# Rotary scores on one core: stores of 128 rows split into 112, 15 and 1 rows in half of the steps, with k's transposes moved late

## The chip, the cores and the metric

The kernel runs on one core of one Trainium2 chip. The time is the device time of the whole program in microseconds (us), as the median of its runs. Spans in profiles are about 1.8 us shorter than times. The ratios are taken over fast runs of both kernels; they differ a little from the ratio of the medians quoted beside them.

## The reference, cut to what matters

```python
batch, seq, heads, dim = 16, 512, 16, 64          # fp32 throughout
q_rot = concat([q1 * cos - q2 * sin, q1 * sin + q2 * cos])   # the halves of dim; k likewise
scores = np.einsum('bshd,bthd->bsht', q_rot, k_rot)
```

The last line means: `out[b, s, h, t]` is the product of the rotated q at (s, h) with the rotated k at (t, h). The output has 16 x 512 x 16 x 512 fp32 numbers, 268 MB, and q and k are 67 MB together. So the kernel is mostly a matter of writing.

## The kernel before

There are 64 steps, four for each batch. A step computes the scores of 128 positions: VectorE rotates q and k, TensorE transposes them and multiplies, ScalarE copies the scores from PSUM into a staging tile of 128 rows by 32 KB, and one DMA issued by SyncE stores the tile. There are three staging tiles.

```python
stage_pool = ctx.enter_context(tc.tile_pool(name="stage", bufs=3))
# ... cut ...
def scores(i, p, st):
    # ... cut: two matmuls into ps ...
    nc.scalar.copy(out=st[:, 2 * p : 2 * p + 2, :], in_=ps)
    if b == 0 and p % 2 == 1:                       # the first four steps: in quarters
        nc.sync.dma_start(o_v[0, c, :, G * i : G * (i + 1)], st[:, G * c : G * (c + 1)])
    elif b > 0 and p == HP - 1:                     # the other 60 steps: one DMA of 128 rows
        nc.sync.dma_start(o_v[b, i % C], st)
# ... cut ...
for i in range(C, NST):
    # ... cut: load of a later pair of q or k ...
    for p in range(HP):
        scores(i, p, st)
        if p in (0, 2, 3, 5) and tr:                # k's transposes first, then q's
            bank, dst = transposed(*tr.pop(0))
            run(dve[:1]); dve = dve[1:]
            nc.vector.tensor_copy(out=dst, in_=bank)
```

## Time and profile before

| | before |
|---|---|
| time, median of 2 | 811.86 us (811.51 to 812.21) |
| span of the profiled run | 810.0 us |
| bytes moved by SyncE's DMA queue | 335.55 MB, its packets fill 98.1% of the 16 DMA engines' span |
| TensorE busy | 676.1 us (83%) |
| mean rate | 415 GB/s |

The third and fourth rows say what to read first: the DMA engines have no room (98.1%), every compute engine has some (the busiest, TensorE, is at 83%). The page counts 16 DMA engines, and the trace holds 16 completion records for each of the 148 DMAs of this kernel. I read each record as one engine's, so the spread of the 16 shows how far the engines have drifted apart. Each packet has a duration too. Both kinds of records are in the trace.

### The profile page before, as it was taken

How to read it: one execution, taken by the hardware profiler on the slowest of the kernel's cores; microseconds unless marked ns; L12 is line 12 of the kernel's file. 1: busy time of each engine (PE TensorE's matmuls, PEld its weight loads, DVE VectorE, ACT ScalarE, POOL GpSimd, SP SyncE). 2: the span in 40 equal slices, each digit the busy share in tenths (PEclk: the TensorE clock that was granted, in tenths of full speed). 3: DMA queues.
4: the chain of work that ended last, by engine and by line, in shares of the span. 5: the costliest groups of instructions: out<-in, count | busy, mean ns of one | idle time of the engine just before them, and what ended most of it. 6: DMA issues, size and time to landing. Idle time of an engine off the chain costs nothing.

```text
span 810.0 us, 7781 instructions
## 1 busy us (share of the span) xinstructions
PE 676.1 (83%) x3072; PEld 297.1 (37%) x3072; DVE 598.7 (74%) x624; ACT 500.1 (62%) x533; POOL 0.7 (0%) x6
## 2 busy tenths in 40 slices
PE   4997999888887888978888888888888889889960
PEld 2443444333333333333333333333333334334310
DVE  7798988877777877868868688677778787786300
ACT  3884777656565675566666656665656657566770
POOL 0000000000000000000000000000000000000000
PEclk9998999999999999999999999999999999999995
DMA  8999999999999999999999999999999999999994
GB/s 272 383 424 397 426 428 426 433 418 431 434 424 432 433 422 434 433 421 438 431 420 437 432 420 438 432 420 438 432 417 442 409 421 440 428 386 435 398 417 202
DMA packets 29028, 336.31 MB, mean 415 GB/s; under 512 B 3392, under 2 KB 7744, under 8 KB 15424
## 3 DMA queue, kind: packets, MB, share of 16 engines
q1 hardware_dynamic: 27648, 335.55, 98.1%
q8 instruction: 24, 0.39, 0.2%
q10 hardware_dynamic: 1344, 0.26, 0.2%
q14 instruction: 12, 0.10, 0.0%
HBM read 67.37 MB, written 268.44 MB: 415 GB/s over the span
## 4 chain that ended last, share of the span: by engine, by line
DMA 58%; PE 22%; DVE 8%; ACT 8%; issue 1%; ACTq 0%
DMA out_dram<-st 57%; PE ps L159 16%; ACT st L166 8%; PE bank L136 6%; DVE part L118 3%; DVE k_rot L121 2%; DVE k_rot L115 1%; DVE q_rot L121 1%; DVE q_rot L115 1%; DVE qT_t L259 1%; DMA sin_k<-in_sin_dram 1%; DVE kT_t L215 0%; ACT kT_t L176 0%; ACTq L286 0%; ACTq L166 0%
## 5 line engine op out<-in xcount | busy, mean ns | idle before, releaser
L166 ACT COPY st<-ps 128x1024 f32<-128x1024 f32 x512 | 488.9, 1022 | 275.0 <-DMA out_dram<-st 176.4
L159 PE MATMUL ps<-kT_t,qT_t 64*128 64x512 f32 x2048 | 528.0, 637 | 72.1 <-ACT st L166 69.4
L159 PEld LDWEIGHTS ps<-kT_t,qT_t 64*128 64x128 f32 x2048 | 183.6, 194 | 255.3 <-issue 148.3
L259 DVE COPY qT_t<-bank 128x512 f32<-128x512 f32 x118 | 81.6, 691 | 135.7 <-PE bank L136 135.1
L136 PE MATMUL bank<-ident,k_rot 128*128 128x128 f32 x512 | 84.6, 291 | 35.7 <-DVE k_rot L121 35.6
L136 PEld LDWEIGHTS bank<-ident,k_rot 128*128 128x128 f32 x512 | 55.1, 143 | 132.7 <-DVE k_rot L121 69.0
L136 PEld LDWEIGHTS bank<-ident,q_rot 128*128 128x128 f32 x512 | 58.4, 149 | 99.8 <-issue 74.8
L259 DVE COPY kT_t<-bank 128x512 f32<-128x512 f32 x112 | 77.0, 688 | 24.2 <-PE bank L136 24.2
L136 PE MATMUL bank<-ident,q_rot 128*128 128x128 f32 x512 | 90.0, 304 | 1.9 <-DVE q_rot L121 1.9
L121 DVE TENSOR_TENSOR k_rot<-k_rot,part 128x1024 f32<-128x1024 f32 x64 | 78.4, 1224 | 2.1
L115 DVE TENSOR_TENSOR q_rot<-q_sb,cos_q 128x1024 f32<-128x1024 f32 x64 | 78.0, 1219 | 0.0
L121 DVE TENSOR_TENSOR q_rot<-q_rot,part 128x1024 f32<-128x1024 f32 x64 | 77.8, 1216 | 0.2
L118 DVE TENSOR_TENSOR part<-q_sb,ss_q 128x1024 f32<-128x1024 f32 x64 | 77.8, 1216 | 0.0
L115 DVE TENSOR_TENSOR k_rot<-k_sb,cos_k 128x1024 f32<-128x1024 f32 x64 | 77.8, 1216 | 0.0
L118 DVE TENSOR_TENSOR part<-k_sb,ss_k 128x1024 f32<-128x1024 f32 x64 | 77.8, 1216 | 0.0
L176 ACT COPY kT_t<-bank 128x512 f32<-128x512 f32 x10 | 5.6, 619 | 6.6 <-PE bank L136 6.6
L215 DVE COPY kT_t<-bank 128x512 f32<-128x512 f32 x6 | 4.1, 685 | 4.5 <-PE bank L136 4.5
L176 ACT COPY qT_t<-bank 128x512 f32<-128x512 f32 x10 | 5.6, 618 | 2.6 <-PE bank L136 2.6
L59 DVE COPY ss_k<-sin_k 128x128 f32<-128x128 f32 x1 | 0.2, 227 | 5.3 <-DMA sin_k<-in_sin_dram 5.3
L176 ACT ACT_TABLE_LOAD x1 | 1.3, 1283 | 2.9 <-issue 2.9
masks.py:199 POOL TENSOR_SCALAR_AFFINE_SELECT ident<-ident 128x128 f32<-128x128 f32 x1 | 0.3, 292 | 0.1
L60 DVE TENSOR_SCALAR ss_q<-sin_q 128x128 f32<-128x128 f32 x1 | 0.2, 222 | 0.0
(7 smaller groups left out, 1.0 us busy)
## 6 DMA issues: line engine op xcount, KB each, us to landing
out_dram<-st SPq DMA_DIRECT2D x60, 4096.0 KB, 28.1
k_sb<-in_k_dram SPq DMA_DIRECT2D x30, 1024.0 KB, 19.1
q_sb<-in_q_dram SPq DMA_DIRECT2D x30, 1024.0 KB, 27.2
out_dram<-st SPq DMA_DIRECT2D x16, 1024.0 KB, 9.9
k_sb<-in_k_dram SPq DMA_DIRECT2D x4, 512.0 KB, 7.0
q_sb<-in_q_dram SPq DMA_DIRECT2D x4, 512.0 KB, 8.4
cos_k<-in_cos_dram ACTq DMA_DIRECT2D x1, 64.0 KB, 4.2
sin_k<-in_sin_dram ACTq DMA_DIRECT2D x1, 64.0 KB, 4.1
```

The costliest lines, as they stand in the source:

```text
L59: nc.vector.tensor_copy(out=ss[:, :, 0, :], in_=tabs["sin", which])
L60: nc.vector.tensor_scalar_mul(ss[:, :, 1, :], tabs["sin", which], -1.0)
L115: lambda: nc.vector.tensor_tensor(a.rearrange(v1, **k1), src.rearrange(v1, **k1), cs, op=mult),
L118: lambda: nc.vector.tensor_tensor(bt.rearrange(v1, **k2), src.rearrange(v1, **k2), ss, op=mult),
L121: lambda: nc.vector.tensor_tensor(a4, a4, swapped, op=add),
L136: nc.tensor.transpose(bank[:, x, :], src, ident)
L159: nc.tensor.matmul(out=ps[:, r, :], lhsT=lhs[64 * r : 64 * r + 64, :], rhs=rhs[64 * r : 64 * r + 64, :], start=True, stop=True,)
L166: nc.scalar.copy(out=st[:, 2 * p : 2 * p + 2, :], in_=ps)
L176: nc.scalar.copy(out=dst, in_=bank)
L215: nc.vector.tensor_copy(out=dst, in_=bank)
L259: nc.vector.tensor_copy(out=dst, in_=bank)
```

## The change

The name of the change says that it comes on top of another one, "k's transposes late and moved by ScalarE". Four things differ. The first loads go into a staging-sized tile of their own in larger pieces, and more loads are issued at the start. The sine tables are built by ScalarE. k's transposes come late in a step and ScalarE copies them out. And in 33 of the 60 whole stores (steps 12 to 44) rows 0 to 111 are stored by SyncE, rows 112 to 126 by GpSimd, and row 127 by two DMAs of 16 pieces of 1 KB. The aim of the last part is probably to take a row off one of the 16 DMA engines: the trace has one packet of 32 KB a row, so the 112 rows could be 7 for each, and the 15 packets of GpSimd's DMA leave at least one engine without one.

```diff
+    MIXED = range(12, 45)
+    early = stage_pool.tile([P, 2 * C * H * D], fp32, tag="stage", name="early")
 ...
+    def store(o, st, mixed):
+        if not mixed:
+            nc.sync.dma_start(o, st)
+            return
+        n = P - 16
+        nc.sync.dma_start(o[:n], st[:n])
+        nc.gpsimd.dma_start(o[n : P - 1], st[n : P - 1])
+        o = o[P - 1 :].rearrange("p h (x t) -> p x h t", x=2)
+        last = st[P - 1 :].rearrange("p h (x t) -> p x h t", x=2)
+        for x in range(2):
+            nc.sync.dma_start(o[:, x], last[:, x])
 ...
-            nc.sync.dma_start(o_v[b, i % C], st)
+            store(o_v[b, i % C], st, i in MIXED)
 ...
-            tr = []
+            tr = {}
+            if i + 1 < NST:
+                tr[1], tr[3] = ("q", i + 1, 0), ("q", i + 1, 1)
             if i + C < NST:
-                tr += [("k", i + C, g) for g in range(2)]
+                tr[5], tr[6] = ("k", i + C, 0), ("k", i + C, 1)
 ...
+                if tr[p][0] == "q":
+                    nc.vector.tensor_copy(out=dst, in_=bank)
+                else:
+                    nc.scalar.copy(out=dst, in_=bank)
```

More of the change, by code (lines that the diff above doesn't have):

```diff
@@ L58, in build_table @@
         ss = const_pool.tile([P, C, 2, HD], fp32, name=f"ss_{which}")
-        nc.vector.tensor_copy(out=ss[:, :, 0, :], in_=tabs["sin", which])
-        nc.vector.tensor_scalar_mul(ss[:, :, 1, :], tabs["sin", which], -1.0)
+        nc.scalar.copy(out=ss[:, :, 0, :], in_=tabs["sin", which])
+        nc.scalar.mul(ss[:, :, 1, :], tabs["sin", which], -1.0)
         tabs["ss", which] = ss.rearrange("p c x j -> p c (x j)")
@@ L71, in in_tile, with load_units @@
         return t
-    def load_unit(which, u):
-        t = in_tiles.get((which, u // 2))
-        if t is None:
-            t = in_tile(which, u // 2)
-        src = (k_v if which == "k" else q_v)[0, :, :, G * u : G * (u + 1), :]
-        nc.sync.dma_start(t[:, u % 2].rearrange("p (c h d) -> p c h d", c=C, h=G), src)
+    st_first = [stage_pool.tile([P, H, S], fp32, tag="stage", name="st") for _ in range(2)]
+    early = stage_pool.tile([P, 2 * C * H * D], fp32, tag="stage", name="early")
+    units = {}
+    def load_units(which, head, heads):
+        n = C * heads * D
+        t = early[:, load_units.used : load_units.used + n]
+        load_units.used += n
+        t = t.rearrange("p (c e) -> p c e", c=C)
+        src = (k_v if which == "k" else q_v)[0, :, :, head : head + heads, :]
+        nc.sync.dma_start(t.rearrange("p c (h d) -> p c h d", d=D), src)
+        for h in range(0, heads, G):
+            units[which, (head + h) // G] = t[:, :, D * h : D * (h + G)]
+    load_units.used = 0
     def load_pair(which, pair):
@@ L92, in rope @@
     def rope(which, n):
-        src = in_tiles[which, n // 2][:, n % 2]
         a = rot_pool.tile([P, H * D], fp32, tag="rot_" + which, name=which + "_rot")
@@ L99, in rope @@
         if n < C:
+            src = units[which, n]
+            sv = "p c (g j) -> p c g j"
             v1 = "p (c g j) -> p c g j"
@@ L105, in rope @@
         else:
+            src = in_tiles[which, n // 2][:, n % 2]
+            sv = "p (g j) -> p g j"
             v1 = "p (g j) -> p g j"
@@ L115, in rope @@
             lambda: nc.vector.tensor_tensor(
-                a.rearrange(v1, **k1), src.rearrange(v1, **k1), cs, op=mult
+                a.rearrange(v1, **k1), src.rearrange(sv, j=HD), cs, op=mult
             ),
             lambda: nc.vector.tensor_tensor(
-                bt.rearrange(v1, **k2), src.rearrange(v1, **k2), ss, op=mult
+                bt.rearrange(v1, **k2), src.rearrange(sv, j=D), ss, op=mult
             ),
@@ L184 @@
         load_tables("q", "(p c) j -> p c j")
-        for u in range(2):
-            load_unit("k", u)
-            load_unit("q", u)
-        for which in ("k", "q"):
-            for u in range(2, C):
-                load_unit(which, u)
+        for head, heads in ((0, G), (G, H - G)):
+            load_units("k", head, heads)
+            load_units("q", head, heads)
         load_pair("k", 2)
+        load_pair("q", 2)
+        load_pair("k", 3)
         make_identity(nc, ident)
         build_table("k")
+        build_table("q")
         run(rope("k", 0))
         tr_act("k", 0)
-        build_table("q")
         run(rope("q", 0))
@@ L201 @@
         for i in range(C):
-            st = stage_pool.tile([P, H, S], fp32, tag="stage", name="st")
+            st = st_first[i] if i < 2 else stage_pool.tile([P, H, S], fp32, tag="stage", name="st")
             late = []
@@ L207 @@
                 dve = rope("k", i + 1) + rope("q", i + 1) + rope("k", C + i)
+                nxt = [("k", i + 1), ("q", i + 1)]
             else:
                 dve = rope("q", C) + rope("k", C + i) + rope("q", C + 1) + rope("k", 2 * C)
+                nxt = [("q", C), ("k", C + i)]
             for p in range(HP):
                 scores(i, p, st)
-                if p in (1, 2) and late:
+                if p in (0, 1) and late:
                     bank, dst = transposed(*late.pop(0))
@@ L215 @@
                     nc.vector.tensor_copy(out=dst, in_=bank)
-                if p == 5:
-                    run(dve[: 3 if i == 0 else 1])
-                    dve = dve[3 if i == 0 else 1 :]
-                    tr_act(*(("k", i + 1) if i < C - 1 else ("q", C)))
-                if p == 7:
-                    run(dve[:3])
-                    dve = dve[3:]
-                    tr_act(*(("q", i + 1) if i < C - 1 else ("k", C + i)))
-            run(dve)
-            if i == 0:
-                load_pair("k", 3)
-                load_pair("q", 2)
-            elif i == 2:
-                load_pair("k", 4)
-                load_pair("q", 3)
+                if i == 0 and p == 1:
+                    load_pair("k", 4)
+                if i == 0 and p == 3:
+                    load_pair("q", 3)
+                if p in (2, 6):
+                    m = len(dve) - (6 if p == 2 else 3) + (-3 if i == C - 1 else 0)
+                    run(dve[:m])
+                    dve = dve[m:]
+                    tr_act(*nxt.pop(0))
+            run(dve)
+            if i == 1:
                 load_pair("k", 5)
@@ L237 @@
         for i in range(C, NST):
-            tr = []
+            tr = {}
+            if i + 1 < NST:
+                tr[1], tr[3] = ("q", i + 1, 0), ("q", i + 1, 1)
             if i + C < NST:
-                tr += [("k", i + C, g) for g in range(2)]
-            if i + 1 < NST:
-                tr += [("q", i + 1, g) for g in range(2)]
+                tr[5], tr[6] = ("k", i + C, 0), ("k", i + C, 1)
             dve = []
@@ L247 @@
                 dve += rope("k", i + 1 + C)
+            st = stage_pool.tile([P, H, S], fp32, tag="stage", name="st")
+            for p in range(HP):
+                scores(i, p, st)
+                if p not in tr:
+                    continue
+                bank, dst = transposed(*tr[p])
+                if tr[p][0] == "q":
+                    run(dve[:1])
+                    dve = dve[1:]
+                    nc.vector.tensor_copy(out=dst, in_=bank)
+                else:
+                    nc.scalar.copy(out=dst, in_=bank)
+            run(dve)
             if i % 2 == 1:
@@ L251 @@
                 load_pair("k", (i + 4) // 2 + 3)
-            st = stage_pool.tile([P, H, S], fp32, tag="stage", name="st")
-            for p in range(HP):
-                scores(i, p, st)
-                if p in (0, 2, 3, 5) and tr:
-                    bank, dst = transposed(*tr.pop(0))
-                    run(dve[:1])
-                    dve = dve[1:]
-                    nc.vector.tensor_copy(out=dst, in_=bank)
-            run(dve)
 _INS = ['q', 'k', 'cos', 'sin']
```

## The prediction

> **What bounds the kernel now.** I read the page first, then the chain of waits, the waits of SyncE's queue, the timeline of the start, and the completion records of the DMAs. The page:
>
> ```profile
> span 810.0 us, 7781 instructions
> PE 676.1 (83%) x3072; PEld 297.1 (37%) x3072; DVE 598.7 (74%) x624; ACT 500.1 (62%) x533; POOL 0.7 (0%) x6
> ...
> GB/s 272 383 424 397 426 428 426 433 418 431 434 424 432 433 422 434 433 421 438 431 420 437 432 420 438 432 420 438 432 417 442 409 421 440 428 386 435 398 417 202
> ...
> q1 hardware_dynamic: 27648, 335.55, 98.1%
> ...
> DMA 58%; PE 22%; DVE 8%; ACT 8%; issue 1%; ACTq 0%
> DMA out_dram<-st 57%; PE ps L159 16%; ACT st L166 8%; PE bank L136 6%; DVE part L118 3%; DVE k_rot L121 2%; DVE k_rot L115 1%; DVE q_rot L121 1%; DVE q_rot L115 1%; DVE qT_t L259 1%; DMA sin_k<-in_sin_dram 1%; DVE kT_t L215 0%; ACT kT_t L176 0%; ACTq L286 0%; ACTq L166 0%
> ...
> L166 ACT COPY st<-ps 128x1024 f32<-128x1024 f32 x512 | 488.9, 1022 | 275.0 <-DMA out_dram<-st 176.4
> ...
> out_dram<-st SPq DMA_DIRECT2D x60, 4096.0 KB, 28.1
> ```
>
> The reader should see a kernel bound by its transfers. SyncE's queue q1 fills the DMA engines for 98.1% of the span; PE has only 83%. The copies into the staging tile wait 176.4 us in all for stores to leave, so compute is ahead. A store lands 28.1 us after its issue, so more than two steps of transfers are always queued. The rate is low only at the start (272, 383, 397 GB/s in slices one, two and four) and in the last slice.
>
> The average hides which DMA engine is last. Each DMA leaves 16 completion records, one for each engine. I took, for each DMA, the first of them and how far the others lag. For the 4 MB store issued at 79.90 us, all 16 come within 0.3 us. At 340 us the latest engine lags by 8.8 us, at 626 us by 14.6 us, and for the last store the first engine ends at 798.8 us, thirteen within 2 us, one 5.6 us later and one 10.2 us later, at 809.0. So the end is set by one engine. It falls back almost only in stores, by about 0.25 us each: some 6% of the 32768-byte packets (one in sixteen) take about 1247 ns where the rest take 1213. Eight packets by 34 ns by 60 stores is 16.3 us. A second engine falls back irregularly, 9 to 11 us by mid-run. Three staging buffers absorb a spread of about 14 us; from 640 us the fast engines therefore run dry now and then.
>
> Then the start:
>
> ```profile
> 19.59 6.81 SPq L169 DMA_DIRECT2D out_dram<-st  x4
> ...
> 62.30 16.81 SPq L88 DMA_DIRECT2D k_sb<-in_k_dram  x2
> ...
> 66.82 1.09 PE L136 MATMUL bank<-ident,k_rot 128*128 128x128 f32 x4 [4.31 <-DVE k_rot L121]
> ...
> 79.90 0.36 SPq L171 DMA_DIRECT2D out_dram<-st  x1
> ```
>
> These are start, duration, engine, line. The loads of the start have landed by 19 us, before the first store's data flow; and at 66.8 us PE waits 4.3 us for VectorE's rotation of k, which makes the first whole store late (79.90).
>
> [...]
>
> **The change part by part.**
>
> 1. Work of one fast engine before, by the spacing of its completions: 60 stores of 9.69 us, 16 quarter stores of 2.46, 30 loads of q of 2.44, 30 of k of 2.50, 8 small loads of 1.50 make 581.4 + 39.4 + 73.2 + 75.0 + 12.0 = 781.0 us. First data flow at about 2.7 us (4.18 less 1.50). That is 783.7; the fast engines end at 798.8, so they were idle some 15 us: 6.9 by the gaps between completions until 84 us (2.8 at 18 to 23, 0.7, 0.2 and 0.6 until 37, 2.2 at 79 to 84, 0.4 after) and some 7.4 after 640 us.
>
> 2. The small loads. Six of the eight are joined to two of 1.5 MB with runs of 3 KB instead of 1 KB. 1 KB runs cost 1.50 us for 512 KB (349 GB/s), longer ones 1.25. So 12.0 becomes about 3.0 + 7.4: 1.6 us saved for every engine (estimate).
>
> 3. Loads fetched earlier. 7 MB instead of 5 MB are issued before the first store, and two more among the first stores. Counting 2.46 us a MB: loads until 21 us, with the first store issued near 19.6; stores and loads until 36, 48, 58 and 73 us. The loads no longer leave a hole at 18 to 23 us.
>
> 4. k's transposes late, copied by ScalarE. In the first whole step PE no longer stands before the k rotation (4.3 us and the slow restart after it), so the store of 79.90 should be issued at 73 to 75. Of the 6.9 us idle at the start about 1 stays: 5.9 saved. In steady state it removes 112 copies of 0.69 us from VectorE and adds as many of 0.6 to ScalarE: 70 us, 500 to about 570 busy. A step then costs ScalarE about 9.0 us and PE 10.6, against 12.1 of transfers (one store and one load); before, an unblocked step took 10.5 us (store issues at 90.39 and 100.88). This lies beside the transfers and is worth nothing there. The loads move behind the store of the step, later by part of a step, which the queue hides.
>
> Without the mixed store, the late engine still ends it: 811.9 - 1.6 - 5.9 = 804.4 us.
>
> 5. The mixed store, 33 times. If the slow engine is the one spared, it moves 7 rows of 8: 33 x 1.247 = 41 us less. Each engine, the slow one too, gets two 1 KB pieces (46 ns each) and three more completion descriptors (9 ns): 0.12 us, 4.0 in all. The slow engine then has 37 us to spare against a lag of 18: more than enough, so the second-late engine takes the end. Its sum is 781.0 - 1.6 + 2.7 + 1 (idle) + 4.0 + 11 (its lag) + 1 (receipt) = 799.1 us of span, and 1.8 more as a time (811.9 against 810.0): 801 us. [...]**Prediction: 803 us.**
>
> **The rivals.**
>
> [...]If each mixed store cost only one row more, 1.21 x 33 = 40 us would be added: 843[...]. Against: the engines drift apart[...], and somebody chose half of the steps on purpose. One time in nine.
>
> *The spared engine is not the slow one.* The slow engine gets the pieces as well: 804.4 + 4 = 808. Nothing in the trace numbers it.
>
> *The lag of the second engine is chance or goes away.* Its steps of 0.3 to 1.4 us come mostly while loads run; instruction fetches of 16 KB (24, up to 1.05 us each) hit single engines too. If all engines end together, 801 - 8 = 793, which would be faster by over 2% (below 795.6).
>
> *Compute becomes the bound.* PE has 10.6 us busy in a step of 12.1; its clock averages 0.95. With transfers 2% shorter, 11.9 us a step still hold it.
>
> **Range and chances.** Most ways lie between 793 and 810[...]. Range 793 to 820. Faster by over 2% needs nearly perfect balance: 0.13. Slower needs over 828[...]: 0.10. Within: 0.77.
>
> **What would show it.** Step 2 and 3: no hole in the completions at 18 to 23 us, slice two above 410 GB/s. Step 4: the first whole store issued before 76 us, ScalarE 565 to 575 busy. Step 5: the latest of the 16 completions of the last whole stores within 6 us of the first instead of 10 to 14; a GpSimd queue with some 16 MB (33 x 480 KB); copies still waiting for stores. Wrong: packets of 32768 bytes well above 1213 ns in steps 12 to 44 and the step there above 12.3 us[...], or one engine still 10 us late (another engine was spared).

Passages that told of the hardware what no trace or run of this case shows are cut, and the cuts marked, here and in the expectations below. The sum in step 5 came to 799.1 us of span and 801 us as a time; the 803 us are these 801 and a term of 2 us that is cut. Of the first rival only its sum (one row more a mixed store, 843 us), two grounds against it and its chance are left; it said that rows read at one time hold each other up, and its reasons were not shown. That a split store spares one engine a row was not shown by a trace of the kernel before. The "slow restart" of step 4 is in the timeline: eight matmuls took 3.79 us from 67.83 us on, and 1.99 us from 74.27 us on.

## The result

The changed kernel takes 988.43 us (984.3 and 992.57) against 811.86. The ratio is 1.2162, with a 95% interval of 1.2049 to 1.2274. It is slower by 177 us.

The page of the changed kernel, the lines that answer to those of before (GB/s is the rate in 40 equal slices of the span; a queue's line has packets, MB and the share of the 16 engines' span; the last two lines have count, KB each and us from issue to landing):

```profile
span 982.5 us, 7913 instructions
PE 731.5 (74%) x3072; PEld 310.0 (32%) x3072; DVE 522.9 (53%) x508; ACT 564.7 (57%) x649; POOL 17.9 (2%) x39
...
GB/s 360 426 432 405 432 433 383 336 314 312 301 276 313 294 285 309 268 302 280 305 292 309 314 313 324 291 295 323 282 335 346 385 422 407 428 408 394 422 389 251
...
q1 hardware_dynamic: 27120, 319.34, 86.9%
q0 software_dynamic: 1056, 16.22, 8.9%
...
DMA 77%; PE 15%; ACT 2%; DVE 2%; SPq 1%; issue 0%; ACTq 0%
...
L193 ACT COPY st<-ps 128x1024 f32<-128x1024 f32 x512 | 497.0, 1019 | 372.8 <-DMA out_dram<-st 262.1
...
out_dram<-st SPq DMA_DIRECT2D x33, 3584.0 KB, 35.2
...
out_dram<-st POOLq DMA_DIRECT2D x33, 480.0 KB, 12.9
```

The rate tells where the time went. After the first slice it is 405 to 433 GB/s until slice six, falls to some 300 while the mixed stores run, and is near 400 again from slice 33. The copies wait longer for stores than before (262.1 us against 176.4). The same stretches as windows, first of the changed kernel, then of the kernel before (start and end, length, busy time and count of each engine, granted clock, share of the DMA engines, GB/s):

```profile
90.00:159.00 69.00, 63.91 (x296) 27.55 (x294) 47.94 (x48) 53.32 (x63) 0.00 (x0) 0.98 1.00 425
200.00:700.00 500.00, 346.74 (x1352) 143.76 (x1352) 229.47 (x224) 250.56 (x284) 14.51 (x28) 0.81 0.95 300
820.00:900.00 80.00, 71.40 (x321) 30.16 (x320) 51.54 (x51) 57.81 (x67) 0.00 (x0) 0.96 0.99 412
```

```profile
90.00:159.00 69.00, 64.01 (x308) 28.28 (x308) 62.03 (x66) 47.82 (x51) 0.00 (x0) 1.00 1.00 426
200.00:700.00 500.00, 428.29 (x1928) 186.94 (x1928) 382.97 (x402) 306.55 (x322) 0.00 (x0) 0.96 1.01 429
```

Outside the mixed steps the two kernels move the same (425 and 426 GB/s). Inside, the engines of the changed kernel are called busy for 95% of the time and move only 300 GB/s instead of 429. So the DMA engines are seldom short of work; their packets take longer. Between 200 and 600 us a packet of 32768 bytes takes 1554 ns on the mean of SyncE's queue, where it took 1216 before, and one in ten takes 2445 ns or more, twice the normal 1213. GpSimd's rows take 2802 ns on the mean, up to 8168. The loss is not spread evenly over the engines either. For the stores of 112 rows issued between 200 and 600 us, the last of the 16 completions comes 23.3 us after the first (median), where it was 9.1 us for the whole stores before. The copies wait for the latest completion: in the kernel before, each of the 51 copies that waited for a store started 99 to 100 ns after the last of its 16 records, 9.7 us after the first (median; 19.5 us in the changed kernel).

The queue lines allow a sum. With plain stores (run x1_plain below) 335.55 MB fill 98.5% of 803.4 us, which is 791 us or 2.36 us a MB. In the changed kernel q1 needs 0.869 x 982.5 = 854 us for 319.34 MB, where 753 would do: 101 us more. q0 needs 87 us for 16.22 MB, where 38 would do: 49 more. The engines are idle for 41 us of the span instead of 12: 29 more. That is 179 us, the difference to the plain stores' span (busy and idle time make up the span, so the sum only shows where it sits).

### The profile page after: what moved, and what is told of

It reads as the page before. It is cut to its first block, busy times and chain, and to the rows that moved or that the text cites. A ratio compares the mean times of both kernels' runs of the same rounds, so it can differ in the third digit from the quotient of the medians.

```text
span 982.5 us, 7913 instructions
## 1 busy us (share of the span) xinstructions
PE 731.5 (74%) x3072; PEld 310.0 (32%) x3072; DVE 522.9 (53%) x508; ACT 564.7 (57%) x649; POOL 17.9 (2%) x39
## 3 DMA queue, kind: packets, MB, share of 16 engines
q1 hardware_dynamic: 27120, 319.34, 86.9%
q0 software_dynamic: 1056, 16.22, 8.9%
## 4 chain that ended last, share of the span: by engine, by line
DMA 77%; PE 15%; ACT 2%; DVE 2%; SPq 1%; issue 0%; ACTq 0%
DMA out_dram<-st 74%; PE ps L186 11%; PE bank L150 4%; DMA q_sb<-in_q_dram 3%; ACT st L193 2%; SPq L174 1%; DVE part L132 1%; DMA cos_k<-in_cos_dram 0%; DVE kT_t L243 0%; DVE q_rot L129 0%; DVE q_rot L135 0%; DVE k_rot L135 0%; DVE k_rot L129 0%; ACTq L314 0%; SPq L168 0%
## 5 line engine op out<-in xcount | busy, mean ns | idle before, releaser
L186 PE MATMUL ps<-kT_t,qT_t 64*128 64x512 f32 x2048 | 579.9, 681 | 200.6 <-ACT st L193 200.6
L193 ACT COPY st<-ps 128x1024 f32<-128x1024 f32 x512 | 497.0, 1019 | 372.8 <-DMA out_dram<-st 262.1
L186 PEld LDWEIGHTS ps<-kT_t,qT_t 64*128 64x128 f32 x2048 | 190.1, 206 | 405.6 <-ACT st L193 263.6
L150 PEld LDWEIGHTS bank<-ident,q_rot 128*128 128x128 f32 x512 | 64.7, 162 | 120.3 <-issue 102.1
L150 PE MATMUL bank<-ident,q_rot 128*128 128x128 f32 x512 | 99.7, 328 | 2.6 <-DVE q_rot L135 2.6
L132 DVE TENSOR_TENSOR part<-k_sb,ss_k 128x1024 f32<-128x1024 f32 x60 | 73.0, 1217 | 0.0
L283 ACT COPY kT_t<-bank 128x512 f32<-128x512 f32 x112 | 66.8, 596 | 10.0 <-PE bank L150 9.9
L169 POOL DMA_DIRECT2D out_dram<-st x33 | 17.2, 522 | 702.6 <-ACT st L193 702.6
L129 DVE TENSOR_TENSOR k_rot<-early,cos_k 128x1024 f32<-128x1024 f32 x4 | 4.9, 1220 | 4.9 <-DMA cos_k<-in_cos_dram 4.9
L203 ACT COPY kT_t<-bank 128x512 f32<-128x512 f32 x10 | 5.5, 605 | 2.1 <-PE bank L150 2.1
L243 DVE COPY kT_t<-bank 128x512 f32<-128x512 f32 x6 | 4.1, 686 | 2.7 <-PE bank L150 2.7
L132 DVE TENSOR_TENSOR part<-early,ss_k 128x1024 f32<-128x1024 f32 x4 | 4.9, 1218 | 0.0
L129 DVE TENSOR_TENSOR q_rot<-early,cos_q 128x1024 f32<-128x1024 f32 x4 | 4.9, 1217 | 0.0
```

The lines of the kernel that those rows point to most:

```text
L129: lambda: nc.vector.tensor_tensor(a.rearrange(v1, **k1), src.rearrange(sv, j=HD), cs, op=mult),
L132: lambda: nc.vector.tensor_tensor(bt.rearrange(v1, **k2), src.rearrange(sv, j=D), ss, op=mult),
L150: nc.tensor.transpose(bank[:, x, :], src, ident)
L169: nc.gpsimd.dma_start(o[n : P - 1], st[n : P - 1])
L186: nc.tensor.matmul(out=ps[:, r, :], lhsT=lhs[64 * r : 64 * r + 64, :], rhs=rhs[64 * r : 64 * r + 64, :], start=True, stop=True,)
L203: nc.scalar.copy(out=dst, in_=bank)
```

## The experiments

Three theories were put to the test first. P: which rows of the staging tile are read at one time decides how long their packets take. Q: more DMAs in flight make SyncE wait, so the engines run dry. G: GpSimd's own path is slow. In all runs but x1_plain and x15_plain_again only the function `store` differs from the changed kernel, and the 33 steps are the same; in those two no step is mixed. All 15 runs are below. Versions marked "wrong result" store the wrong rows. Where an expectation has lost the condition before its first figure, the figure is the one for P; the sizes expected for P were not shown by any trace before.

### x1_plain and x15_plain_again: without the mixed store

```diff
-    MIXED = range(12, 45)
+    MIXED = ()
```

> The changed kernel with every whole store issued as one 128-row DMA by SyncE, so only the other parts of the change are left. All three theories ([...]Q: more DMAs in flight make SyncE wait and starve the engines; G: GpSimd's own DMA path is slow) agree here: 804 us, 798 to 810, with the first whole store issued before 76 us and about 1 us idle among the DMA engines until 84 us. If it is over 900, the loss lies in none of the three but in k's transposes or the loads.

> The changed kernel with plain stores once more, in five rounds, because 808.8 against 811.7 us (ratio 0.9983, 0.9945 to 1.0021) leaves open whether it beats the kernel before. All theories: 803 to 810 us, ratio 0.990 to 1.000.

Measured: 808.76 us (805.2 to 813.65, 4 runs) against 811.73, ratio 0.9983 (0.9945 to 1.0021); again 809.2 us (805.5 to 810.45, 6 runs) against 811.79, ratio 0.9958 (0.9930 to 0.9987). So all of the loss lies in the mixed store, and what is left of the change is worth some 0.4% (the second interval lies under 1). It is the only version with a right result that beats the kernel before, by little; I take its time as 809 us below. The page of x1_plain:

```profile
span 803.4 us, 7719 instructions
...
GB/s 345 420 417 435 387 425 434 420 442 423 425 436 432 422 438 427 429 434 425 429 434 429 431 429 425 439 425 427 433 431 428 431 431 427 429 405 393 405 427 219
...
q1 hardware_dynamic: 25536, 335.55, 98.5%
```

### x2_only112: the 112 rows alone

```diff
         nc.sync.dma_start(o[:n], st[:n])
-        nc.gpsimd.dma_start(o[n : P - 1], st[n : P - 1])
-        ... the two DMAs of pieces
```

> Wrong result on purpose: in the 33 mixed steps only rows 0 to 111 are stored, by one DMA of SyncE; no GpSimd, no pieces, and 17 MB less to write (33 x 512 KB, some 40 us at 430 GB/s). Q and G: 804 - 40 = 764 us. P: [...]the 112 rows take as long as 128 or longer: 804 us or more, and packets of 32768 bytes in those steps have a mean well above 1216 ns.

Measured: 866.54 us (865.67 and 867.41), wrong result. Some 58 us more than the plain stores with 17 MB less to write, so about 98 us for the 33 DMAs of 112 rows, 3.0 us each. Neither GpSimd nor extra DMAs are there to blame. Packets of 32768 bytes take 1468 ns on the mean (200 to 600 us). Its span and queue:

```profile
span 863.9 us, 7719 instructions
...
q1 hardware_dynamic: 25008, 318.25, 95.6%
```

### x3_halves and x5_mid: the same output rows from other staging rows

```diff
+        nc.sync.dma_start(o[:64], st[:64])      # x3_halves
+        nc.sync.dma_start(o[64:], st[64:])
...
+        nc.sync.dma_start(o[:64], st[32:96])    # x5_mid, wrong result
+        nc.sync.dma_start(o[64:], st[32:96])
```

> In the 33 mixed steps the store is two DMAs of SyncE of 64 rows each; no GpSimd, no pieces[...]. Q: one DMA more a step, within 10 us of the plain one. G: as the plain one, 804. P: [...]up to 9.7 us more a mixed step: 33 x 9.7 = 320, some 1000 to 1130 us, and packets of 32768 bytes of about 2400 ns.

> Wrong result on purpose: as the two halves, but both DMAs read staging rows 32 to 95; the output rows written, the bytes, the number and shape of the DMAs are those of the halves (903 us). Only the rows of SBUF differ[...]. [...]back to the plain store, 803 to 815 us, 32768-byte packets at 1216 ns. If the collision is in HBM (which rows of the output are written at once) or is the price of a DMA of 64 rows: about 900 us as the halves.

Measured: x3_halves 903.06 us (899.73 and 906.38), x5_mid 809.91 us (809.4 and 810.41). The page of x3_halves and its window, then those of x5_mid:

```profile
span 897.9 us, 7785 instructions
...
q1 hardware_dynamic: 26064, 335.56, 97.9%
...
200.00:600.00 400.00, 313.76 (x1274) 130.53 (x1272) 215.07 (x210) 230.83 (x263) 0.00 (x0) 0.87 0.99 352
```

```profile
span 807.6 us, 7785 instructions
...
q1 hardware_dynamic: 26064, 335.56, 98.3%
...
200.00:600.00 400.00, 346.31 (x1538) 145.70 (x1536) 262.46 (x256) 278.68 (x321) 0.00 (x0) 0.95 1.01 429
```

The number of packets, the bytes, the shape of the DMAs and the addresses written are equal; only the rows of SBUF that are read differ. That alone makes 352 or 429 GB/s, and packets of 1462 or 1217 ns. It rules out HBM, the size of 64 rows and the number of DMAs. Nor is x5_mid fast because it reads fewer different rows: the plain stores read all 128 at 430 GB/s. The runs show that the choice of rows decides; why these rows are slower together they do not show. x3_halves missed its expectation, though: it costs 2.9 us a mixed step, not the 9.7 (about a whole store's 9.69 us) that were given as the most. A likely reason, not tested, is that the engines do not run in step: the completions of one such store lie 16 to 18 us apart (median), more than a plain step takes (12.35 us), so while some engines read the rows of one store, others are already in another.

### x4_columns and x8_no_pieces: the waits of SyncE

```diff
+        for x in range(4):                      # x4_columns: 128 rows, four heads each
+            nc.sync.dma_start(o[:, 4 * x : 4 * x + 4], st[:, 4 * x : 4 * x + 4])
...
         nc.sync.dma_start(o[:n], st[:n])        # x8_no_pieces: last row not stored
         nc.gpsimd.dma_start(o[n : P - 1], st[n : P - 1])
-        ... the two DMAs of pieces
```

> In the 33 mixed steps the store is four DMAs of SyncE of 128 rows and four heads each: as many DMAs in a step as the changed kernel has[...]. P and G: as the plain one within 8 us (804). Q: the wait of SyncE for earlier DMAs shows as in the changed kernel and the time is 900 us or more.

> Wrong result on purpose: 112 rows by SyncE, 15 by GpSimd, the last row not stored at all. If the two DMAs of pieces cost what their packets show (49 ns each, 4 us in all): 975 to 990. If the pieces, by SyncE's waits before them or by all engines reading one row, are a main cost: 940 or less.

Measured: x4_columns 816.84 us (816.32 and 817.36), x8_no_pieces 994.58 us (991.84 and 997.32). The changed kernel does have a new wait: SyncE stands for earlier stores before it may issue more. In the waits of SyncE's queue (total, times, longest) the changed kernel shows

```profile
SPq L168 <- DMA out_dram<-st: 186.1, 30, 15.2
```

and x4_columns

```profile
SPq L168 <- DMA out_dram<-st: 206.4, 95, 6.9
```

So the same kind of wait, longer in total, costs 8 us where every DMA reads all 128 rows. In x8_no_pieces SyncE issues the 112 rows and the load alone in a step, and the only wait for earlier stores left in its queue is the one at the end of the program:

```profile
SPq L308 <- DMA out_dram<-st: 20.7, 3, 9.6
```

The time is not shorter. Q falls, and the pieces with it: their packets take 49 ns.

### x9_pool_whole and x13_heads: GpSimd with all 128 rows

```diff
+        nc.gpsimd.dma_start(o, st)                       # x9_pool_whole
...
+        nc.sync.dma_start(o[:, :14], st[:, :14])         # x13_heads
+        nc.gpsimd.dma_start(o[:, 14:], st[:, 14:])
```

> In the 33 mixed steps the whole 128-row store is issued by GpSimd as one DMA[...]. [...]803 to 820 us. If GpSimd's own path[...] is slow: 840 or more.

> In the 33 mixed steps SyncE stores heads 0 to 13 of all 128 rows and GpSimd heads 14 and 15 of all 128 rows, so GpSimd moves an eighth of the bytes as in the changed kernel, its packets come between SyncE's[...]. [...]805 to 825 us. If mixing two queues on an engine costs by itself (976 against 944 us for the 16 rows by GpSimd and by SyncE): 835 or more.

Measured: x9_pool_whole 818.24 us (813.62 and 822.86), x13_heads 820.25 us (817.01 and 823.49). GpSimd can store all 128 rows, or an eighth of each, at 9 to 11 us more than SyncE in 33 steps. So where every DMA reads all 128 rows G is worth about 0.3 us a step, out of 5.4 (two runs each, up to 9 us apart). Beside 112 rows it may be worth more, see x11_pool16 next.

### x6_sp112_16, x7_no_pool and x11_pool16: who issues the last 16 rows

```diff
+        nc.sync.dma_start(o[112:], st[112:])             # x6, beside the 112 rows
...
-        nc.gpsimd.dma_start(o[n : P - 1], st[n : P - 1]) # x7: pieces kept
+        nc.sync.dma_start(o[n : P - 1], st[n : P - 1])
...
+        nc.gpsimd.dma_start(o[112:], st[112:])           # x11, beside the 112 rows
```

> In the 33 mixed steps 112 rows and then 16 rows, both by SyncE; no GpSimd, no pieces. Against the 112 rows alone (867 us) this adds 33 x 512 KB, 40 us of transfers. If the 16 rows cost only their bytes: 907 us, and then the remaining 80 us of the changed kernel come from GpSimd or the pieces. If the 16 rows collide[...]: 940 to 1030 us. I expect 950.

> The changed kernel with the 15 rows issued by SyncE too. [...]960 to 1010, as with GpSimd (988). GpSimd's path slow: about 910, as the other rows alone cost. If it is more than 1010, GpSimd's early rows were a help.

> 112 rows by SyncE and 16 rows by GpSimd; with 944 us for both by SyncE. If GpSimd makes it worse (its rows come between those of earlier stores): 980 to 1000, as with 15 rows (995). If it is the number 15 that is worse: about 944.

Measured: x6_sp112_16 943.83 us (948.45 and 939.21), x7_no_pool 974.44 us in the one fast run (the other, 996.63, is slow), x11_pool16 975.77 us (972.83 and 978.71). The 16 rows cost 77 us when SyncE issues them, twice their bytes, and 109 when GpSimd does. So beside the 112 rows GpSimd adds 32 us, 1.0 us a step; x11 came just under the 980 to 1000 expected for that. x7's one fast run is 14 us below the changed kernel's 988.43; fast runs of one split version differ by up to 9 us (x6_sp112_16), so one run does not resolve that. Either way GpSimd is not the main cause: without it 165 of the 179 us remain.

### x12_spread15 and x14_aligned108: what the 15 rows cost by themselves

```diff
         nc.sync.dma_start(o[:112], st[:112])             # x12, wrong result
+        nc.gpsimd.dma_start(o[112:127], st[32:92:4])
...
+        nc.sync.dma_start(o[:64], st[32:96])             # x14, wrong result
+        nc.sync.dma_start(o[64:108], st[32:76])
+        nc.gpsimd.dma_start(o[108:123], st[112:127])
```

> Wrong result on purpose: as the 112 rows by SyncE and 15 by GpSimd without the last row (995 us), but the 15 rows are read from staging rows 32, 36, ... 88[...]. [...]867 + 38 = 905, up to 930. If GpSimd's DMA costs it in another way: above 970.

> Wrong result on purpose: SyncE stores staging rows 32 to 95 and then 32 to 75 (64 and 44 rows[...]), GpSimd the 15 rows 112 to 126[...]. [...]809 + 33 x 1.21 = 849 us if the 15 rows cost only their bytes. If 15 rows[...] cost as much as they seem to in the changed kernel (995 against 867 us, that is 128 us): 900 or more. Then the large cost of the 15 rows is their own; near 849 it is that they fall among 112 rows[...].

Measured: x12_spread15 959.94 us in the fast run (993.71 in the slow one), x14_aligned108 962.32 us (958.1 and 966.54). x12 missed its expectation of 905 to 930 and rests on one fast run. GpSimd's rows did become quick (1640 ns on the mean, against 2917 in x8_no_pieces), but they still cost 93 us above the 112 rows alone, against 128 in x8_no_pieces. Those 15 rows are among the rows that SyncE's DMA reads at the same time, so x12 may have paid on that side what it saved on the other; this was not tested, and x12 settles nothing alone. x14 goes on from the rows that cost nothing in x5_mid: beside rows 32 to 95 and 32 to 75, rows 112 to 126 by GpSimd cost 153 us, 4.6 us a step. The expectation allowed 1.2 us of this for one row more on an engine, an estimate from the 1213 ns of a packet. That would leave 113 us, 3.4 us a step. But the DMAs of 44 rows left 12 completion records each instead of 16, and no run has them without the 15 rows; nor were the 15 rows tried beside these stores from other staging rows or by SyncE. So the parts of the 44 rows and of GpSimd in the 3.4 us are not separated. Its page:

```profile
span 956.3 us, 7847 instructions
...
q1 hardware_dynamic: 25239, 313.93, 81.2%
q0 software_dynamic: 1056, 16.22, 12.6%
```

GpSimd's 16.22 MB take 0.126 x 956.3 = 120 us here instead of 38. Its packets have a median of 3954 ns, 3.3 times the 1213 of a row alone.

### x10_spare15: is the spared engine the late one?

```diff
+        nc.sync.dma_start(o[:60], st[32:92])             # wrong result
+        nc.sync.dma_start(o[60:120], st[32:92])
```

> Wrong result on purpose: in the 33 mixed steps rows 32 to 91 of the staging tile are stored twice, by two DMAs of SyncE of 60 rows, so fifteen engines get four rows each[...], and the sixteenth gets none. The fifteen have as much to do as in the plain store. If the sixteenth is the engine that lags: its completions come early, the spread at the end falls under 6 us and the time to 796 to 803. If another engine is the late one: the spread of 9 to 14 us stays and the time is about 808, as the plain one.

Measured: 810.67 us (808.16 and 813.18), as the plain stores. In the 33 steps one of the 16 completions of each 60-row store comes 0.5 to 1.3 us after its issue, and the other fifteen follow 5.6 to 28 us after it: one engine, it seems, has no rows. Yet the spread among the fifteen stays (median 11.1 us). For the store issued at 248.58 us, twelve land 17 to 21 us after the idle one and three 26 us after it; for the one of 559.79 us, twelve at 12 to 15 us, two at 22 and the last at 27. So the engine left out by a split into fifteen is not the one that ends last. Which number either has, the trace does not say, nor whether GpSimd leaves out the same one for its 15 rows.

## Why the prediction was wrong

The predicted 803 us and the range of 793 to 820 both missed 988.43.

**What bounds the kernel before, and steps 1 to 4.** These held in kind. The changed kernel's first whole store is issued at 71.71 us (predicted 73 to 75), and x1_plain's at 73.12:

```profile
71.71 0.34 SPq L165 DMA_DIRECT2D out_dram<-st  x1
```

ScalarE is busy for 564.7 us (predicted 565 to 575). Slice two has 426 GB/s (above 410). The first loads of batch 0 end at 14.4 us in x1_plain, against 15.5 before: 1.2 us saved where 1.6 were estimated. The loads and stores follow each other without the hole at 18 to 23 us. The figure of 804.4 us for the version without the mixed store compares with 805.2 us for the run that was profiled and 809 us in the median. The fast engines end at 793.3 us instead of 798.8, 5.5 us earlier where 7.5 were worked out, and the late engine still comes 9.3 us after them. So this part of the mechanism was right, and its size was some 5 us too large in the median (7.5 us worked out, 2.7 measured). Its sums are right.

**Step 5 failed**: "Each engine, the slow one too, gets two 1 KB pieces (46 ns each) and three more completion descriptors (9 ns): 0.12 us, 4.0 in all", with the 2 us added. A mixed store costs (988.4 - 809) / 33 = 5.4 us instead of 0.18 (6 us by 33). The pieces were priced well (49 ns, and their removal saved nothing), and so were the packets of 4 bytes, 16 to a DMA (9 ns). What was priced wrong is the rows that stay. Stores of all 128 rows, or of rows 32 to 95 twice, ran at 430 and 429 GB/s (x1_plain, x5_mid), those of rows 0 to 63 and 64 to 127 at 352 (x3_halves), the mixed ones at 300 (the changed kernel). When rows were counted by engine, it was taken for granted that it does not matter which rows they are. The 112 rows cost about 3.0 us a store over their bytes (x2_only112). The 15 rows cost about 4.6 us by x14_aligned108 (with whatever its 44 rows cost), 3.9 us beside the 112 rows (994.6 less 866.5, by 33). Both figures for the 15 rows include their own bytes, some 1.2 us a step (16.22 MB at 2.36 us a MB, by 33).

**The rival was named and mispriced.** The first rival counted one row more a store, 40 us, and was given one chance in nine. It priced one row alone, "if each mixed store cost only one row more", and gave the worst case no price: GpSimd's packets took a median of 3954 ns in x14_aligned108, more than three times a row's 1213. Of the grounds set against it, that "the engines drift apart" may have been right in part: x3_halves paid 2.9 us of the 9.7. That "somebody chose half of the steps on purpose" is no measurement of the profile.

**The rival of the spared engine** is supported as well: x10_spare15 shows that a split into fifteen leaves out an engine that is not the late one. Had the choice of rows cost nothing, the mixed store would have won nothing by that evidence, at least when issued by SyncE. In the changed kernel itself the sign "within 6 us" failed too: the completions of the whole store issued at 896.00 us, after the mixed steps, lie 12.7 us apart, those of the last one 8.7 us. So the term "33 x 1.247 = 41 us less" did not show either.

**The other signs of step 5** came as listed: packets of 32768 bytes well above 1213 ns in steps 12 to 44, GpSimd's queue with 16.22 MB, a mixed step of 17.7 us (the 33 stores of 112 rows are issued from 159.5 to 724.7 us), against 12.35 in the same steps of x1_plain.

**What stays open.** 16 rows cost 32 us more by GpSimd than by SyncE beside the 112 rows; x13_heads, 11 us above the plain stores, bounds what two queues cost where every DMA reads all 128 rows; the rest was not separated. Which engines fall behind in the mixed steps, the trace does not say. Why the choice of rows matters is not shown either: no record names a packet's rows. Why one engine is slower by some 34 ns a packet in stores is not known.

## What to carry to other kernels

The stores that ran at the full rate here read all 128 rows, or rows 32 to 95 (430 and 429 GB/s; rows 0 to 63 and 64 to 127 gave 352); before splitting such a transfer by rows, measure which rows are read at one time, not only count them by engine. Splitting by columns keeps all 128 rows and was nearly free here (8 us in 33 steps); splitting by rows was free with rows 32 to 95 (x5_mid, wrong result) and cost 94 to 179 us in the versions that split by rows and stored every row. When a rival theory is written down, work out its worst case with the same care as the favourite's, and give its chance by that.
